# Gate table of a PEER layer built by 8 tokens instead of 4, with its products in alternating row blocks and one copy per PSUM bank

## The chip, the cores and the metric

One core of one Trainium2 chip runs the whole kernel. The metric is device time in microseconds; the time of a kernel is the median of its runs.

## The reference

One inference step of a two-layer encoder for 256 prompt rows and 128 sample rows of width 1024. Layer 0 mixes with a short gated convolution, layer 1 with stick-breaking attention; after each follows a PEER channel mixer, and every sub-layer ends in a layer norm. What matters here is PEER, for 256 rows at a time:

```python
q = (xb @ w_q).reshape(PEER_BLOCK, PEER_HEADS, 2, PEER_HALF)
s = jnp.einsum("thpc,hpnc->thpn", q, subkeys)
s_top, i_top = lax.top_k(s, K)
cand = s_top[:, :, 0, :, None] + s_top[:, :, 1, None, :]
cand_idx = i_top[:, :, 0, :, None] * PEER_N_KEYS + i_top[:, :, 1, None, :]
best, pos = lax.top_k(cand.reshape(PEER_BLOCK, PEER_HEADS, K * K), K)
expert = jnp.take_along_axis(cand_idx.reshape(...), pos, axis=-1)
g = jax.nn.softmax(best, axis=-1)
act = jax.nn.gelu(jnp.einsum("td,thkd->thk", xb, u_tab[expert]), approximate=False)
return jnp.einsum("thk,thkd->td", g * act, v_tab[expert])
```

Each token has 8 heads with 16 experts each, so 128 chosen experts of 16384, numbered 128 x + y by a first key x and a second key y.

## The kernel before, in words

The 128 sample rows and the 256 prompt rows take two ways through the same engines. For the sample rows the chosen experts' rows are gathered from HBM (`peer_gather`, L354, L367, L372: a gather by GpSimd, then one pass of VectorE over each gathered tile of 128 x 1024). For the prompt rows all 16384 experts are computed, and a gate is zero where a token has not chosen the expert (`peer_dense`). Both run at the same time, and the sample rows' work fills VectorE and the DMA queues beside the prompt rows' work.

`peer_dense` has three stages in each of the two layers. First, 14 pairs of blocks of 128 experts get their first product early, while VectorE does the routing (`a_pair`, from L382). Second, the gate table G is built (L407 to L437); this is the stage that the change rewrites. Third, for 64 pairs of blocks, the first product, the gate's product (`wt`, L457) and the second product follow, with float32 operands split in two parts.

The gate table. G[j, group, t, i] is the gate of token t for expert (group * 16 + i, j). It is built from one-hot rows: with the 128 chosen experts of a token on the partitions, `oi` is the gate where i equals x and zero elsewhere, `oj` is one where j equals y, and `oj`^T `oi` sums them into 128 x 128 gates of one token. The comparisons come from products: TensorE forms i - x and (j - y)^2 for 4 tokens at a time as products with 18 rows of contraction (L422): `xj` holds x, y and two parts of y^2 of 4 tokens and two rows of ones, `near` the matching coefficients. The 18 rows lie in one of four blocks of 32 rows; q = t0 // 64 * 32 is that block, so 16 successive groups of 4 tokens use the same one. Each of the two products fills one PSUM bank of the pool `acc` (4 banks). VectorE makes `oi` from the first (L424), ScalarE `oj` from the second (L427), both from a PSUM bank of 512 columns. Four float32 products of 128 columns (L430), one for each token, fill a bank of the pool `pg` (2 banks); the profile has two records for each of them. Two ScalarE copies empty it: the first four groups go into G (L432), the last four into the tile `st` (L435; pool `ohp`, 3 buffers), which after every 8 tokens is stored to `Gd` in DRAM by the SP queue (L437). In the third stage, when G's first groups have been used, L459 reloads them from Gd.

`xj` is filled in `route_prompt`: the keys of one tile of 128 tokens go to DRAM (`xd`, L342) and come back, transposed, by two DMAs for each tile (L345).

The order. The code is written in program order, and the framework's scheduler decides at build time in which order each engine issues its instructions (`schedule_with_timeline_sim=True`): of what is ready by its own timing it takes what stands first in the program. A tile's slot in a pool is given out when an earlier user of it is done. On the chip each engine then works in that fixed order. The sample rows' attention is given a place in that order by `ranked`.

Of the kernel before, what the change touches and what calls it, by code (L numbers as in the profile page):

```python
# [18 lines left out]
P = 128  # L19
# [8 lines left out]
# those of them with (a + 1)(b + 1) <= 8, as (a's start and count, b's count): only they can be among the best 8  # L28
# [4 lines left out]
EARLY = 14  # pairs of blocks whose first product precedes the gates  # L33
KEEP = 4  # of them in SBUF until they are used, the others in DRAM
AHEAD = 4  # blocks by which the first product runs ahead of the second
# [3 lines left out]
def trunk(ctx: ExitStack, tc: tile.TileContext, I, O):  # L39
# [31 lines left out]
    with ExitStack() as es:  # L71
# [19 lines left out]
        # trig[k', k] = 1 where k' >= k  # L91
        nc.vector.tensor_scalar(trig, jp, 0.0, None, op0=OP.is_le)
        nc.vector.memset(ones, 1.0)
        # same[p, j] = 1 where p and j lie in the same block of 16
# [3 lines left out]
        # maskb[k, q]: 0 where k < q and both lie in the same block, else NEG or less  # L98
# [6 lines left out]
    def split(hi, lo, src):  # L105
        """src = hi + lo exactly, each of float32r's 12 significant bits"""
        nc.scalar.activation(hi, src, AF.Copy)  # L107
        return nc.vector.tensor_sub(lo, src, hi.bitcast(F32))  # L108
# [7 lines left out]
    def in_turn(this, that):  # L116
        """this behind that on their engine, which so changes its tables of functions less often"""
        tc.add_manual_dep(this.ins, that.ins.name, mybir.DependencyInfo(
            mybir.DependencyClass.NoSync, mybir.DependencyReason.SCHED_ONLY), reason="fewer loads of tables")
# [25 lines left out]
    def mm3(pt, L, R, first, last):  # L145
        """pt (+)= L^T R for operands in two parts"""
# [4 lines left out]
    def proj3(pt, w, hT, n):  # L151
        """pt[:, :n] = w^T hT, w: parts of 8 chunks of 128x128, hT: parts [128, 8, n]"""
        for c in range(NB):
            cs = slice(c * P, (c + 1) * P)
            mm3(pt[:, :n], [x[:, cs] for x in w], [x[:, c, 0:n] for x in hT], c == 0, c == NB - 1)

    def proj1(pt, w, hT):
        """pt = w^T hT in float32"""
# [34 lines left out]
    def transposed(r, dsts, ps):  # L193
        """write r^T into each of dsts (parts (hi, lo) [128, 8, 128], or one float32 tile)"""
# [15 lines left out]
    def topk_half(chains, small):  # L210
        """the 16 best of s [128, 128] and their places, in order; step by step for all chains (tv, ti, n, s)"""
# [12 lines left out]
    def stage2(tv, ti, al, g, e, nh=8):  # L224
        """experts e [128, 8, 16] (float32) and softmax gates g [128, 8, 16] of the 16 best pairs of each head.
        Only the pairs (a, b) with (a + 1)(b + 1) <= 16 can be among them: the others have 16 before them.
        tv: the best keys' values, and room behind them for as many numbers of keys"""
        # kind and head in one dimension: sums of values, then numbers of experts
# [29 lines left out]
        for k0, x, pl in ((0, ex8, places8), (8, ex, places)):  # L258
# [3 lines left out]
            # the numbers once for each rank, side by side  # L262
# [12 lines left out]
        # the sums of the cells: ever again the first half onto the second, in front of an odd one out  # L275
# [18 lines left out]
    def softmax(g, sm):  # L294
        """of each head's values less their maximum"""
# [5 lines left out]
    def from_pool(pl):  # L301
        """shapes count words of 4 bytes"""
        return lambda name, shape, dt=F32: pl.tile([P] + shape[:-1] + [shape[-1] * 4 // mybir.dt.size(dt)], dt, name=name)

    def from_arena(ar, start=0):
        """places in ar one after the other"""
# [13 lines left out]
    def route_prompt(tv, ti, al, xj, xd, gT, t):  # L320
        """of the 128 experts of tile t's tokens: the first keys x and the second keys y, as rows x, y and y^2 in two
        parts of 7 bits of every token, 4 tokens to a group and 16 groups to a block of 32 rows, into xj; the gates,
        into gT [128 k, 256 t]"""
# [19 lines left out]
        for b in range(2):  # L343
            p = (2 * t + b) * 32
            nc.sync.dma_start(xj[p:p + 16], xd[t, b * 64:b * 64 + 64].rearrange("(s r) (q k) -> (r q) s k", r=4, q=4))  # L345
# [5 lines left out]
    def gather(tab, ei, k):  # L351
        """rows of tab for the k-th experts of all tokens"""
# [26 lines left out]
    def peer_dense(L, hT, dn):  # L379
        """-> psum banks [2 tiles * 2 halves] of the sum over the experts"""  # L380
        lag, kept, early = {}, {}, {}

        def a_pair(i, pl, ps, native=False):
            """gelu(u h) of two blocks, with or without splitting u"""
# [11 lines left out]
        # some pairs while VectorE is busy with the routing  # L396
# [16 lines left out]
        # gates G[j, group, t, i] of the experts (group * 16 + i, j); the last four groups wait in DRAM  # L413
        G = dn.gp.tile([P, 4, TP, GI], F32, name="G")
        Gd = dram.tile([P, 4, TP, GI], F32, name="Gd")
        for t0 in range(0, TP, 4):
            us = slice(t0, t0 + 4)
            # i - x and (j - y)^2 of all places in a row and column, for 4 tokens
            q = t0 // 64 * 32
            px, pj = bank(acc), bank(acc)  # L420
            for k, pt in enumerate((px, pj)):
                nc.tensor.matmul(pt, lhsT=xj[q:q + 18, t0 % 64 // 4, :], rhs=near[q:q + 18, k, :], start=True, stop=True)  # L422
            oi = ohp.tile([P, 4, P], F32, name="oi")
            nc.vector.scalar_tensor_tensor(oi, px.rearrange("p (t i) -> p t i", i=P), 0.0,  # L424
                                           gT[:, us, None].to_broadcast([P, 4, P]), op0=OP.is_equal, op1=OP.mult)
            oj = ohp.tile([P, 4, P], F32, name="oj")
            nc.scalar.activation(oj.rearrange("p t j -> p (t j)"), pj, AF.Relu, bias=1.0, scale=-1.0)  # L427
            pt = bank(pg)
            for t in range(4):
                nc.tensor.matmul(pt[:, t * P:(t + 1) * P], lhsT=oj[:, t, :], rhs=oi[:, t, :], start=True, stop=True)  # L430
            ptv = pt.rearrange("p (t h g i) -> p h g t i", h=2, g=4, i=GI)
            nc.scalar.activation(G[:, :, us, :], ptv[:, 0], AF.Copy)  # L432
            if t0 % 8 == 0:
                st = ohp.tile([P, 4, 8, GI], F32, name="st")
            nc.scalar.activation(st[:, :, t0 % 8:t0 % 8 + 4, :], ptv[:, 1], AF.Copy)  # L435
            if t0 % 8 == 4:
                nc.sync.dma_start(Gd[:, :, t0 - 4:t0 + 4, :], st)  # L437
# [6 lines left out]
        for s in range(-AHEAD, NBLK, 2):  # L444
# [12 lines left out]
            nc.vector.tensor_mul(wt, lag.pop(s), G[:, g % 4, :, i:i + 2].rearrange("p t i -> p i t"))  # L457
            if i == GI - 2 and g < 4:
                nc.sync.dma_start(G[:, g], Gd[:, g])  # L459
# [3 lines left out]
            # the last two blocks by tiles, so that the first tile's normalization starts early  # L463
# [7 lines left out]
    def finish(pts, L_ln, hd, last, hT, hTf=None):  # L471
        """residual and layernorm of the two prompt tiles"""
        # the table of square roots, before the data is there
# [30 lines left out]
    def half_out(xT, name, n):  # L504
        """columns n * 512.. of x @ w, in psum"""
# [8 lines left out]
    def attn_sample(h):  # L514
        with ExitStack() as es:
# [8 lines left out]
            # block-diagonal queries [2 x 64 dims, (b, head, q)], and the mask in that order of columns  # L524
# [18 lines left out]
            # two pairs of heads at a time; columns of a pair: keys of the cache, new keys  # L543
# [366 lines left out]
```

## Time and profile before

| | us |
|---|---|
| median of 3 runs | 2388.8 (2382.14 to 2390.61) |
| span of the profiled execution, first to last instruction | 2374.8 |
| PE busy in it | 2271.8 |
| VectorE (DVE) busy | 1918.5 |
| ScalarE (ACT) busy | 1050.3 |

The list of times does not say which of them was the profiled execution; its own time is read from its span. PE is TensorE's matmuls, PEld its weight loads, SP the engine that issues most DMAs, L422 line 422 of the kernel. A matmul's record has a modelled end, so the start of the next is the surer number. DMA share is the mean busy share of 16 DMA engines.

### The profile page before, as it was taken

The page shows a single profiled execution, that of the slowest core. Times are in us where ns is not written, and L with a number is a line of the kernel's source. Part 1 is how long each engine was busy: PE and PEld are TensorE (multiplying, and loading weights), DVE is VectorE, ACT ScalarE, POOL GpSimd, SP SyncE. Part 2 cuts the span into 40 slices and gives each one's busy share as a digit, 9 for nine tenths or more (in the row PEclk, how much of TensorE's full clock was granted, in tenths as well). Part 3 has the DMA queues.
Part 4 walks back from the last instruction along what each step waited for, and adds up shares of the span by engine and source line. Part 5 has one row for each costly group of instructions (what it writes and reads, how often), then busy time and mean ns, then how long its engine had stood idle before and what let it go on. Part 6 is the DMA issues. An engine that isn't in the chain of part 4 may idle for free.

```text
span 2374.8 us, 37270 instructions
## 1 busy us (share of the span) xinstructions
PE 2271.8 (96%) x13708; PEld 1981.6 (83%) x13708; DVE 1918.5 (81%) x3493; ACT 1050.3 (44%) x1579; POOL 800.2 (34%) x659
## 2 busy tenths in 40 slices
PE   8979989999999999998799888988999999999997
PEld 8969876688888889887589677876698888888986
DVE  6559997898888889888623489987898888888888
ACT  3333325744444444443346432135644444444443
POOL 0002342353332343444221223443453332344442
PEclk9989998999999999999899999998999999999999
DMA  4556898999999999998976558989999999999996
GB/s 163 195 193 212 291 339 265 299 369 347 346 325 327 341 330 323 335 335 289 332 243 206 162 194 298 337 287 292 294 373 342 347 329 325 341 320 329 335 326 220
DMA packets 225928, 704.13 MB, mean 297 GB/s; under 512 B 24912, under 2 KB 59472, under 8 KB 224720
## 3 DMA queue, kind: packets, MB, share of 16 engines
q1 hardware_dynamic: 137200, 382.93, 45.3%
q0 software_dynamic: 87968, 318.28, 38.5%
q8 instruction: 108, 1.77, 0.3%
q14 instruction: 76, 0.62, 0.1%
q10 hardware_dynamic: 576, 0.52, 0.1%
HBM read 671.17 MB, written 30.48 MB: 295 GB/s over the span
## 4 chain that ended last, share of the span: by engine, by line
PE 80%; DVE 12%; DMA 5%; issue 2%; ACT 1%; POOL 0%; SPq 0%; DVEq 0%; ACTq 0%; POOLq 0%
PE acc L148 13%; PE acc L149 13%; PE acc L147 13%; PE pg L147 8%; PE pg L149 8%; PE pg L148 8%; PE pg L430 6%; PE ms L160 3%; PE acc L422 3%; DVE row L367 2%; DMA row<-in_pu,ei 2%; DMA row<-in_pv,ei 1%; PE ms L511 1%; DVE h L372 1%; DMA wv<-in_pvn 1%
## 5 line engine op out<-in xcount | busy, mean ns | idle before, releaser
L354 POOL DMA_INDIRECT row<-in_pv,ei x256 | 387.6, 1514 | 580.7 <-DVE h L372 448.4
L354 POOL DMA_INDIRECT row<-in_pu,ei x256 | 333.6, 1303 | 544.6 <-DVE row L367 409.4
L147 PE MATMUL pg<-hThi,uhi 128*128 128x256 f32 x1600 | 451.6, 282 | 0.0
L149 PE MATMUL pg<-hThi,ulo 128*128 128x256 f32 x1600 | 451.4, 282 | 0.0
L148 PE MATMUL pg<-hTlo,uhi 128*128 128x256 f32 x1600 | 451.3, 282 | 0.0
L108 DVE TENSOR_TENSOR vlo<-wv,vhi 128x1024 fp32r<-128x1024 f32 x280 | 341.9, 1222 | 89.4 <-ACT vhi L107 86.0
L107 ACT ACTIVATE vhi<-wv 128x1024 fp32r<-128x1024 f32 x280 | 295.3, 1055 | 259.9 <-PE acc L149 187.1
L148 PE MATMUL acc<-vlo,whi 128*128 128x512 f32 x1024 | 403.9, 394 | 0.1
L149 PE MATMUL acc<-vhi,wlo 128*128 128x512 f32 x1024 | 403.4, 395 | 0.0
L108 DVE TENSOR_TENSOR ulo<-wu,uhi 128x1024 fp32r<-128x1024 f32 x264 | 322.0, 1220 | 100.7 <-ACT uhi L107 91.0
L107 ACT ACTIVATE uhi<-wu 128x1024 fp32r<-128x1024 f32 x264 | 278.9, 1056 | 261.2 <-issue 92.5
L147 PE MATMUL acc<-vhi,whi 128*128 128x512 f32 x1024 | 345.5, 394 | 0.6 <-ACT whi L107 0.6
L372 DVE SCALAR_TENSOR_TENSOR h<-row,wg,h 128x1024 f32<-128x1024 f32 x256 | 327.4, 1279 | 18.7 <-DMA row<-in_pv,ei 18.3
L367 DVE SCALAR_TENSOR_TENSOR row<-row,h 128x1024 f32<-128x1024 f32 x256 | 310.5, 1216 | 13.8 <-DMA row<-in_pu,ei 13.7
L147 PEld LDWEIGHTS pg<-hThi,uhi 128*128 128x128 f32 x1600 | 304.7, 190 | 10.3
L148 PEld LDWEIGHTS pg<-hTlo,uhi 128*128 128x128 f32 x1600 | 304.7, 190 | 8.4
L149 PEld LDWEIGHTS pg<-hThi,ulo 128*128 128x128 f32 x1600 | 304.9, 191 | 5.3
L160 PE MATMUL acc<-arena,wu 128*128 128x256 f32 x1024 | 233.7, 387 | 17.3 <-DMA wu<-in_put 12.3
L160 PEld LDWEIGHTS acc<-arena,wu 128*128 128x128 f32 x1024 | 195.6, 194 | 49.7 <-DMA wu<-in_put 15.8
L149 PEld LDWEIGHTS acc<-vhi,wlo 128*128 128x128 f32 x1024 | 192.5, 188 | 40.3
L148 PEld LDWEIGHTS acc<-vlo,whi 128*128 128x128 f32 x1024 | 193.0, 188 | 37.5 <-DVE vlo L108 0.6
L147 PEld LDWEIGHTS acc<-vhi,whi 128*128 128x128 f32 x1024 | 187.8, 189 | 34.7 <-ACT whi L107 0.8
(261 smaller groups left out, 3244.7 us busy)
## 6 DMA issues: line engine op xcount, KB each, us to landing
wv<-in_pvn SPq DMA_DIRECT2D x256, 512.0 KB, 5.9
wu<-in_put SPq DMA_DIRECT2D x256, 512.0 KB, 6.2
row<-in_wpq POOLq DMA_DIRECT2D x32, 512.0 KB, 4.9
wu<-in_wpq SPq DMA_DIRECT2D x32, 512.0 KB, 5.2
Gd<-st SPq DMA_DIRECT2D x64, 256.0 KB, 5.4
G<-Gd SPq DMA_DIRECT2D x8, 2048.0 KB, 10.6
wu<-in_win SPq DMA_DIRECT2D x24, 512.0 KB, 3.5
early<-lag SPq DMA_DIRECT2D x20, 256.0 KB, 5.8
```

Source lines behind the costliest of these rows:

```text
L107: nc.scalar.activation(hi, src, AF.Copy)
L108: return nc.vector.tensor_sub(lo, src, hi.bitcast(F32))
L147: nc.tensor.matmul(pt, lhsT=L[0], rhs=R[0], start=first, stop=False)
L148: nc.tensor.matmul(pt, lhsT=L[0], rhs=R[1], start=False, stop=False)
L149: nc.tensor.matmul(pt, lhsT=L[1], rhs=R[0], start=False, stop=last)
L160: nc.tensor.matmul(pt, lhsT=w[:, c * P:(c + 1) * P], rhs=hT[:, c, :], start=(c == 0), stop=(c == NB - 1))
L354: nc.gpsimd.indirect_dma_start(out=row, out_offset=None, in_=tab, in_offset=bass.IndirectOffsetOnAxis(ap=ei[k // 32][:, k % 32:k % 32 + 1] ...
L367: nc.vector.scalar_tensor_tensor(u, u, 1.0, h, op0=OP.mult, op1=OP.mult, accum_out=dot[:, k:k + 1])
L372: nc.vector.scalar_tensor_tensor(r, v, wg[:, k:k + 1], r, op0=OP.mult, op1=OP.add)
L422: nc.tensor.matmul(pt, lhsT=xj[q:q + 18, t0 % 64 // 4, :], rhs=near[q:q + 18, k, :], start=True, stop=True)
L430: nc.tensor.matmul(pt[:, t * P:(t + 1) * P], lhsT=oj[:, t, :], rhs=oi[:, t, :], start=True, stop=True)
L511: nc.tensor.matmul(pt, lhsT=xT[:, c + i, :], rhs=w[:, i, :], start=(c + i == 0), stop=(c + i == 7))
```

## The change

The loop over 4 tokens becomes one over 8 tokens. The 4-token groups are dealt out over the four row blocks in turn, so two successive groups lie in different blocks; the loads of `xj` follow this, 4 for each tile instead of 2. All four distance products of the 8 tokens are written one behind the other, and take all four `acc` banks. One copy empties a whole `pg` bank: its output is a pattern of two pieces, the first four groups to their place in G, the last four to spare places for 16 tokens behind G's 256, in turns for even and odd steps. The store to Gd reads from there, and `st` is gone. G and the arena that shares its memory grow by 16 tokens. Comments and doc strings are removed all over the file, which is not shown.

```diff
-        for b in range(2):
-            p = (2 * t + b) * 32
-            nc.sync.dma_start(xj[p:p + 16], xd[t, b * 64:b * 64 + 64].rearrange("(s r) (q k) -> (r q) s k", r=4, q=4))
+        for b in range(4):
+            nc.sync.dma_start(xj[b * 32:b * 32 + 16, t * 8:t * 8 + 8],
+                              xd[t].rearrange("(s b r) (q k) -> b (r q) s k", b=4, r=4, q=4)[b])
...
-        G = dn.gp.tile([P, 4, TP, GI], F32, name="G")
+        G = dn.gp.tile([P, 4, TP + 16, GI], F32, name="G", tag="G")
         Gd = dram.tile([P, 4, TP, GI], F32, name="Gd")
-        for t0 in range(0, TP, 4):
-            us = slice(t0, t0 + 4)
-            q = t0 // 64 * 32
-            px, pj = bank(acc), bank(acc)
-            for k, pt in enumerate((px, pj)):
-                nc.tensor.matmul(pt, lhsT=xj[q:q + 18, t0 % 64 // 4, :], rhs=near[q:q + 18, k, :], start=True, stop=True)
-            oi = ohp.tile([P, 4, P], F32, name="oi")
-            nc.vector.scalar_tensor_tensor(oi, px.rearrange("p (t i) -> p t i", i=P), 0.0,
-                                           gT[:, us, None].to_broadcast([P, 4, P]), op0=OP.is_equal, op1=OP.mult)
-            oj = ohp.tile([P, 4, P], F32, name="oj")
-            nc.scalar.activation(oj.rearrange("p t j -> p (t j)"), pj, AF.Relu, bias=1.0, scale=-1.0)
-            pt = bank(pg)
-            for t in range(4):
-                nc.tensor.matmul(pt[:, t * P:(t + 1) * P], lhsT=oj[:, t, :], rhs=oi[:, t, :], start=True, stop=True)
-            ptv = pt.rearrange("p (t h g i) -> p h g t i", h=2, g=4, i=GI)
-            nc.scalar.activation(G[:, :, us, :], ptv[:, 0], AF.Copy)
-            if t0 % 8 == 0:
-                st = ohp.tile([P, 4, 8, GI], F32, name="st")
-            nc.scalar.activation(st[:, :, t0 % 8:t0 % 8 + 4, :], ptv[:, 1], AF.Copy)
-            if t0 % 8 == 4:
-                nc.sync.dma_start(Gd[:, :, t0 - 4:t0 + 4, :], st)
+        for t0 in range(0, TP, 8):
+            xy = [[bank(acc) for _ in range(2)] for _ in range(2)]
+            for k in range(2):
+                for n in range(2):
+                    q = (t0 // 4 + n) % 4 * 32
+                    nc.tensor.matmul(xy[k][n], lhsT=xj[q:q + 18, t0 // 16, :], rhs=near[q:q + 18, k, :],
+                                     start=True, stop=True)
+            for n in range(2):
+                t1 = t0 + 4 * n
+                oi = ohp.tile([P, 4, P], F32, name="oi")
+                nc.vector.scalar_tensor_tensor(oi, xy[0][n].rearrange("p (t i) -> p t i", i=P), 0.0,
+                                               gT[:, t1:t1 + 4, None].to_broadcast([P, 4, P]),
+                                               op0=OP.is_equal, op1=OP.mult)
+                oj = ohp.tile([P, 4, P], F32, name="oj")
+                nc.scalar.activation(oj.rearrange("p t j -> p (t j)"), xy[1][n], AF.Relu, bias=1.0, scale=-1.0)
+                pt = bank(pg)
+                for t in range(4):
+                    nc.tensor.matmul(pt[:, t * P:(t + 1) * P], lhsT=oj[:, t, :], rhs=oi[:, t, :], start=True, stop=True)
+                there = TP + t0 // 8 % 2 * 8 + 4 * n
+                both = bass.AP(tensor=G.tensor, offset=G[:, 0, t1:t1 + 4, :].offset,
+                               ap=[list(G.ap[0]), [(there - t1) * GI, 2], [(TP + 16) * GI, 4], [1, 4 * GI]])
+                nc.scalar.activation(both, pt.rearrange("p (t h g i) -> p h g t i", h=2, g=4, i=GI), AF.Copy)
+            nc.sync.dma_start(Gd[:, :, t0:t0 + 8, :], G[:, :, there - 4:there + 4, :])
...
-            nc.vector.tensor_mul(wt, lag.pop(s), G[:, g % 4, :, i:i + 2].rearrange("p t i -> p i t"))
+            nc.vector.tensor_mul(wt, lag.pop(s), G[:, g % 4, 0:TP, i:i + 2].rearrange("p t i -> p i t"))
             if i == GI - 2 and g < 4:
-                nc.sync.dma_start(G[:, g], Gd[:, g])
+                nc.sync.dma_start(G[:, g, 0:TP], Gd[:, g])
...
-            self.arena = self.gp.tile([P, 4 * TP * GI], F32, name="arena", tag="G")
+            self.arena = self.gp.tile([P, 4 * (TP + 16) * GI], F32, name="arena", tag="G")
```

## Rows read from the trace of the kernel before

**Rows 1.** The page's first part: busy time, share of the span, instructions.
```profile
span 2374.8 us, 37270 instructions
PE 2271.8 (96%) x13708; PEld 1981.6 (83%) x13708; DVE 1918.5 (81%) x3493; ACT 1050.3 (44%) x1579; POOL 800.2 (34%) x659
```

**Rows 2.** Stretches: length, busy us of each engine, PEclk, DMA share, GB/s.
```profile
400.00:480.00 80.00, 80.00 (x515) 56.28 (x515) 69.21 (x98) 54.87 (x143) 33.39 (x34) 1.00 0.98 300
1645.00:1720.00 75.00, 75.00 (x474) 51.33 (x474) 65.24 (x107) 53.48 (x142) 29.10 (x31) 1.00 0.95 299
```

**Rows 3.** PE in order of time, 429 to 437: start, us, line, form, count.
```profile
431.06 0.60 PE L422 MATMUL acc<-near,xj 18*128 18x512 bf16 x2
431.59 1.16 PE L430 MATMUL pg<-oi,oj 128*128 128x128 f32 x8
432.68 0.60 PE L422 MATMUL acc<-near,xj 18*128 18x512 bf16 x2
```

**Rows 4.** Groups of instructions, 420 to 460: busy us, mean ns, idle before.
```profile
L427 ACT ACTIVATE oj<-acc 128x512 f32<-128x512 f32 x25 | 15.1, 603 | 0.0
L422 PE MATMUL acc<-near,xj 18*128 18x512 bf16 x50 | 14.6, 380 | 0.0
```

**Rows 5.** PE in order of time, prompt attention, around 1184 and 1228.
```profile
1183.98 0.70 PE L667 MATMUL pg<-qkp 64*128 64x256 f32 x2
...
1228.54 0.71 PE L667 MATMUL pg<-qkp 64*128 64x256 f32 x4
```

**Rows 6.** PE in order of time, 395.9 to 399.5.
```profile
395.67 0.37 PE L422 MATMUL acc<-near,xj 18*128 18x512 bf16 x1 [0.32 <-ACT oj L427]
395.97 2.05 PE L430 MATMUL pg<-oi,oj 128*128 128x128 f32 x16
397.95 0.60 PE L422 MATMUL acc<-near,xj 18*128 18x512 bf16 x2
```

**Rows 7.** ACT in order of time, 429 to 437.
```profile
431.16 0.38 ACT L432 ACTIVATE G<-pg 128x256 f32<-128x256 f32 x1 [0.47 <-PE pg L430]
431.44 0.38 ACT L435 ACTIVATE st<-pg 128x256 f32<-128x256 f32 x1
431.71 0.60 ACT L427 ACTIVATE oj<-acc 128x512 f32<-128x512 f32 x1
```

**Rows 8.** All engines in order of time, 369.6 to 370.6.
```profile
369.73 0.60 ACT L427 ACTIVATE oj<-acc 128x512 f32<-128x512 f32 x1
...
370.41 0.50 PEld L430 LDWEIGHTS pg<-oi,oj 128*128 128x128 f32 x2 [0.84 <-ACT oj L427]
```

**Rows 9.** The tile Gd, its 24 stores issued from 400 to 480.
```profile
DMA to landing us min/median/max: 4.3/5.4/6.8
```

**Rows 10.** The stretch 381.6 to 396, columns as in rows 2.
```profile
381.60:396.00 14.40, 14.09 (x62) 9.83 (x60) 8.31 (x11) 6.97 (x19) 3.48 (x4) 0.66 0.56 164
```

**Rows 11.** The tile Gd, its 3 stores issued from 381.6 to 393.
```profile
DMA to landing us min/median/max: 2.6/2.6/2.9
```

**Rows 12.** The line of the xj loads, 340 to 365 (ns min/median/max of issuing).
```profile
L345 SPq DMA_DIRECT2D xj<-xd x4: 319/382/702, 354.9 to 357.9; - x4
  PE acc L422: 1.2, 1
```

**Rows 13.** PE in order of time, 381.5 to 386.8.
```profile
382.07 3.78 PE L430 MATMUL pg<-oi,oj 128*128 128x128 f32 x16
```

**Rows 14.** Stretches early in the stage, columns as in rows 2.
```profile
364.00:374.00 10.00, 10.00 (x36) 6.89 (x36) 6.81 (x9) 5.09 (x12) 1.88 (x2) 0.50 1.03 379
381.20:391.00 9.80, 9.80 (x38) 7.24 (x36) 4.11 (x5) 3.88 (x11) 1.88 (x2) 0.50 0.60 182
```

**Rows 15.** The SP queue's DMA issues at the end: sample rows, then prompt rows.
```profile
2360.10 0.34 SPq L838 DMA_DIRECT2D out_y<-h  x1
2369.59 1.66 SPq L484 DMA_DIRECT2D out_y<-wu  x2
```

## The prediction

> **What bounds the kernel now.** I read the page's summary first, then the table of stretches, then the time order of single engines inside the stage that the change rewrites. The summary has TensorE (PE) busy for nearly all of the span [rows 1]. The stretches show that this holds without a gap where the gate tables are built: PE is busy for all of 80 us in layer 0 and all of 75 us in layer 1, at the full clock, while VectorE (DVE) and ScalarE (ACT) have idle time left [rows 2]. So the question is what one step of this stage costs PE.
>
> PE's time order answers it [rows 3]. For each 4 tokens it shows two distance products (L422), then the 8 records of the four products of one-hot rows (L430; each float32 product leaves two records), then again L422. From one L422 pair to the next is 432.68 - 431.06 = 1.62 us: 0.53 until the first L430 and 1.09 until the next pair. For 8 tokens that is 3.24 us, and nothing in it is a wait: the pair of the next 4 tokens stands ahead of the L430 of these, because four acc banks hold two pairs. 64 steps of 8 tokens (32 in each layer) at 3.24 make 207 us of the span. Only these can move much.
>
> **Removed from PE.** In the new code two L422 that follow each other read different row blocks. The prompt attention in this same trace has both cases [rows 5]: two products in one row block last 0.70 us together, four in two row blocks (the same two, twice) 0.71. The second block rides along. So four L422 should take PE as long as two now, 0.53 to the first L430. The 16 L430 of a step then can stand together. Such a run of 16 exists: from its first to the next L422 is 397.95 - 395.97 = 1.98 us [rows 6]. PE's need is 0.53 + 1.98 = 2.51 for 8 tokens, taken as 2.55, against 3.24. If PE stayed the bound, 64 x 0.69 = 44 us would go. I do not think that it stays the bound.
>
> **Added: a round trip through ACT.** A step now takes all four acc banks. The next step's products get a bank only when `oi` or `oj` of this step has read it, and L430 of this step is ahead of them in program order. Before, the pair that L430 needs was a whole group old. I expect PE to run a step's second pair of L422, wait for `oj`, run 16 L430, and only then run the next such pair. Row by row: L422 0.37 and 0.05 until ACT starts, `oj` 0.60 [rows 4, 7], 0.08 from its end to L430 (369.73 + 0.60 to 370.41) [rows 8], 1.98 for 16 L430: 3.08 us. In ACT's order the last copy of the step before comes first: as now it starts 0.10 after the first L422 [rows 3, 7], and a copy of 512 columns should take what `oj` takes, 0.60. It ends at 0.70, where `oj` wanted to start at 0.42, so up to 0.28 is added: 3.08 to 3.36. PE itself already shows such a wait for `oj` at one place (0.32 before an L422) [rows 6]. The middle, 3.22, is what a step costs now: the side-by-side products are paid back as a wait.
>
> **One copy instead of two.** Two copies of 256 columns start 0.28 apart and take 0.38 each [rows 7], 0.66 together; one of 512 takes 0.60 by `oj`. ACT saves 0.06 for each 4 tokens. ACT is idle for 31% of the stage [rows 2], so I cost this at nothing; if ACT were the limit it would be 8 us. The 512-column copy writes pieces of 256 bytes; no row has just that pattern on ACT, and I bound it between 0.60 and 0.76 (two copies with no overlap).
>
> **Two landing places instead of three.** `st` had three buffers; the 16 spare tokens of G are two. The first copy of a step must wait until the store of two steps before has landed, and everything behind it on ACT, `oj` of the next step included, waits too. The store lands 5.4 us after issue in the median, 4.3 to 6.8 [rows 9]. One place then turns over in 5.4 plus the two copies that fill it (0.60 + 0.49, since ACT starts the next some 0.1 us before the end) plus about 0.07: 6.56 us for two steps, 3.28 for one. At 4.3 it is 2.73, at 6.8 3.98. With three buffers the store had a step more, and no wait shows. Stores land faster only where DMA is little used: 2.6 us in the median [rows 11] at a share of 0.56 [rows 10]; in the stage the share is 0.98 [rows 2], because the sample rows' gathers run on. I take the median.
>
> So a step has two cycles of nearly the same length, 3.22 and 3.28, and the later one wins in each turn; the landings scatter by over 1 us. I take 3.35, a little above both. 64 x (3.35 - 3.24) = 7 us more.
>
> **The smaller edits.** The key table xj is loaded by 8 DMAs instead of 4 in each layer. SP issues one in 0.38 us and PE waited 1.2 us for them in layer 0 [rows 12]; at worst 4 x 0.38 = 1.5 us a layer stand in front of the first product, at best nothing, since the first step needs two of them alone. I take 1 us for both layers. G is 4 KB longer in each partition and `st` is gone: no time. The gate's read and the reload of G only get a limit on tokens: no time, as each touches the same elements.
>
> **Sum.** 7 + 1 = 8 us more. The profiled execution has a span of 2374.8 us; the median of the runs, 2388.8, lies 14.0 above it, which I take as what surrounds a span. 2374.8 + 8 + 14 = **2397 us**.
>
> **One rule against the change.** The rows say that four acc banks hold two pairs now and one step then. The Trainium skill, TensorEngine Tiling (Array Packing), section Restrictions and Gotchas, says the same as a warning: row tiling raises PSUM pressure, since each row tile needs its own bank. The same page, section Performance Considerations, expects the copies out of PSUM to become the bottleneck after the speedup; by that ACT would set the step at 4 x 0.60 = 2.4 us, under PE's 2.55, and the stage would gain. No row here decides between that and the round trip above.
>
> **Rivals.** *Faster (0.27):* the compiled order puts the next products between the two L430 groups of a step, so that `oj` is ready early, and the stores land at the quick end. PE's 2.55 is then held by the places at 2.73: 64 x 0.51 = 33 us less, 2357. For it: order is chosen by a planner, and at 395.97 it put 16 L430 together. Against: banks come free late, and 4.3 is the shortest of 24 landings [rows 9]. A larger gain would meet the sample rows, whose output is issued 9.5 us before the prompt's last [rows 15].
>
> *Slower, the landing places (0.22):* the store's landing decides every step. The point is 2 x 3.24 - 1.16 = 5.3 us; above it the stage is longer than now, and the median is just there. At 6.1, half way to the longest, a step is 3.63: 64 x 0.39 = 25, 2415 with the edits. For it: a late copy holds back `oj` behind it, so that one late landing is not caught up.
>
> *Slower, the clock (0.08):* early in the stage the granted clock fell to half twice, with PE busy by its records [rows 14], and there 16 L430 took 3.78 us instead of 2.05 [rows 6, 13]. With a wait in each step it could fall again. A quarter of the steps at half clock costs 16 x 1.73 = 28 us: 2425. Against: from 400 us on it stayed full. The Trainium skill, TensorE: Matmul & The Clock Gate, section A second HAM failure mode: psum-queue depth-cycling, tells of short PE waits between groups, from cycling through PSUM banks, that make the clock swing; by that rule this rival is the likely one, and the rows of the first 30 us bear it out, those after do not.
>
> *Much slower (0.03):* the framework sees the spare places as one piece, and each copy waits for the store just before: 6.56 a step, 64 x 3.32 = 212, about 2602.
>
> That the products do not run side by side is inside the forecast: PE would need 2.55 + 0.46 = 3.01, still under 3.22.
>
> **The numbers.** Forecast 0.40. A measurement of this kernel can tell about 0.5%, 12 us, from no change: the bounds are 2377 and 2401. Faster 0.27 plus the forecast's lower tail, 0.28; slower 0.22 + 0.08 + 0.03, less a little of the first that stays under 2401, 0.32; same 0.40. The range 2355 to 2432 leaves out the last rival, half of the clock's and the far end of the faster one, some 0.17 together. As both signs have weight: the forecast's own range is 2380 to 2412.
>
> **What would show it.** Right: PE idle for some 0.6 us in each step before L430, released by `oj`; a step of about 3.35 us between first L422s; ACT's copies waiting for the landing of the Gd store; L422 starting in twos. Wrong: PE busy throughout and steps under 3.0 us (faster rival); a step of twice the landing; or copies that never wait for a store, with half clock in the stretches.

## The result and the profile after

The changed kernel takes 2479.3 us in the median of 4 runs (2464.4 to 2482.9), the kernel before 2385.8 beside it: a ratio of 1.0385 with a 95% interval of 1.0348 to 1.0422. It is slower by 93 us, outside the predicted range. The ratios here and below leave out runs more than 1.5% above the fastest run of the same kernel, the medians do not. The page of the changed kernel, against [rows 1]:

```profile
span 2474.8 us, 37201 instructions
PE 2297.4 (93%) x13708; PEld 2016.4 (81%) x13708; DVE 1924.4 (78%) x3493; ACT 1045.5 (42%) x1454; POOL 753.5 (30%) x659
```

The span grew by 100.0 us and PE's busy time by 25.6, so some three quarters of the loss is PE standing still. Where? The distance products mark the two gate stages. The line's own answer has first and last start (fifth and sixth number), layer 0 and then layer 1, first of the kernel before, then of the changed one (L422 is now L423, L430 is L435, the one copy is L439, `oj` L432, `oi` L428, the store L440):

```profile
L422 PE MATMUL acc<-near,xj x128: 371/384/629, 360.1 to 471.4; 18*128 18x512 bf16 x128
L422 PE MATMUL acc<-near,xj x128: 371/384/626, 1599.3 to 1716.3; 18*128 18x512 bf16 x128
```

```profile
L423 PE MATMUL acc<-near,xj x128: 371/384/629, 416.1 to 544.5; 18*128 18x512 bf16 x128
L423 PE MATMUL acc<-near,xj x128: 371/384/629, 1692.7 to 1815.3; 18*128 18x512 bf16 x128
```

Five differences make the 100 us. Until the first product: 360.1 to 416.1, **+56.0**. Layer 0's stage: 111.3 to 128.4, **+17.1**. From there to layer 1's stage: 1127.9 to 1148.2, **+20.3**. Layer 1's stage: 117.0 to 122.6, **+5.6**. The rest: 658.5 to 659.5, +1.0. So 76 us were lost where no changed line of the gate stage runs, most of them before the first one ran.

Stretches before the stage show the place (columns as in [rows 2]), first of the kernel before, then of the changed one, which also has its two stages:

```profile
220.00:240.00 20.00, 19.67 (x170) 19.48 (x170) 20.00 (x97) 5.58 (x13) 6.02 (x9) 1.00 0.56 189
240.00:260.00 20.00, 20.00 (x130) 18.65 (x129) 19.48 (x96) 5.37 (x9) 7.91 (x7) 1.00 0.85 294
360.00:474.00 114.00, 112.26 (x643) 76.25 (x644) 91.83 (x123) 75.05 (x193) 38.32 (x42) 0.91 0.92 281
```

```profile
220.00:240.00 20.00, 1.83 (x7) 1.25 (x6) 18.12 (x65) 1.96 (x5) 11.09 (x11) 0.50 0.83 275
240.00:260.00 20.00, 8.55 (x38) 8.25 (x39) 17.37 (x43) 3.44 (x8) 12.66 (x12) 0.59 0.86 293
416.00:547.00 131.00, 110.91 (x658) 80.63 (x656) 102.51 (x144) 70.36 (x130) 51.86 (x50) 0.87 0.91 289
1693.00:1819.00 126.00, 107.70 (x661) 78.86 (x658) 101.66 (x146) 71.58 (x132) 48.37 (x49) 0.89 0.91 297
```

From 220 to 260 PE was busy for 39.7 of 40 us and is now for 10.4, at half to six tenths of the clock. The longest wait of the changed kernel from 165 to 280 names the cause (sum, times, longest):

```profile
PEld pg L725 <- ACT q L720: 29.8, 2, 24.2
```

L720 copies the prompt rows' queries `q`, from which their keys are chosen. L725 is PE's product of them with the subkeys. PE stands for 24 us waiting for the first of the copies. ACT in order of time shows what had to come first:

```profile
243.97 0.23 ACT L273 ACTIVATE pf<-pos 128x32 bf16<-128x32 uint32 x1 [7.33 <-DVE g L274]
244.21 1.28 ACT L296 ACT_TABLE_LOAD   x1
245.50 0.31 ACT L296 ACTIVATE g<-g 128x128 f32<-128x128 f32 x1
245.72 0.37 ACT L720 ACTIVATE q<-acc 128x256 f32<-128x256 f32 x1
255.44 0.66 ACT L720 ACTIVATE q<-acc 128x256 f32<-128x256 f32 x2 [9.35 <-DVE e L288]
```

L273 and L296 are the end of the *sample* rows' routing, and the prompt rows' `q` needs nothing of its results. The first copy stands behind them in ACT's compiled order. The second waited 9.35 us for L288, which is that routing too. In the kernel before the same copy (L717) started at 169.4 and ran beside the sample rows' routing; this is its row there, then here (copies up to 320 us):

```profile
L717 ACT ACTIVATE q<-acc x16: 364/366/384, 169.4 to 250.7; 128x256 f32<-128x256 f32 x16
```

```profile
L720 ACT ACTIVATE q<-acc x14: 365/367/385, 245.7 to 307.8; 128x256 f32<-128x256 f32 x14
```

What the two share is memory. 16 more tokens make the arena 4 x 16 x 16 x 4 = 4096 bytes longer in each partition, and every pool laid out behind it moves up by as much, `q`'s among them. The temporary pools of the sample rows' routing grow from the other end. In the layout of the built program `q` ended 1152 bytes below them before, and lies over them now. A slot of `q` is then given out when the last user of the tiles under it is done. Under the first slot that is L274, which released L273 above; under the second it is L288. `st` lived in a pool that is opened later, so that its going did not help here.

The stage itself also has other lines than forecast. PE in order of time, in layer 0, and then the copies of the same moments in ACT's order:

```profile
521.59 2.05 PE L435 MATMUL pg<-oi,oj 128*128 128x128 f32 x16 [1.34 <-ACT G L439]
523.57 0.39 PE L423 MATMUL acc<-near,xj 18*128 18x512 bf16 x2
525.00 1.16 PE L435 MATMUL pg<-oi,oj 128*128 128x128 f32 x8 [1.04 <-ACT G L439]
```

```profile
520.94 1.08 ACT L439 ACTIVATE G<-pg 128x512 f32<-128x512 f32 x2 [1.42 <-DMA Gd<-G]
524.35 1.08 ACT L439 ACTIVATE G<-pg 128x512 f32<-128x512 f32 x2 [1.84 <-DMA Gd<-G]
```

Two products in two row blocks last 0.39 us together, where two in one block took 0.60 [rows 3]: they do run side by side. But PE now stands before L435 for 1.34 and 1.04 us, released by the copy, and the copy by the store's landing. Over the stage the waits are:

```profile
ACT oj L432 <- PE acc L423: 31.6, 22, 6.3
PEld pg L435 <- ACT G L439: 14.8, 21, 1.8
ACT G L439 <- DMA Gd<-G: 6.6, 7, 1.8
```

PE is idle for 20.1 of 131 us of the stage and 18.3 of 126, by the stretches; before it was 1.7 of 114 and 9.2 of 120. The mean clock tells the time at half clock as well, twice what it lacks of 1: 2 x 0.13 x 131 = 34 us, against 2 x 0.09 x 114 = 21 before, both in layer 0.

### The profile page after: what moved, and what is told of

Same layout as the page of the kernel before. It is cut to its first block, busy times and chain, and to the rows that moved or that the text cites. A ratio compares the mean times of both kernels' runs of the same rounds, so it can differ in the third digit from the quotient of the medians.

```text
span 2474.8 us, 37201 instructions
## 1 busy us (share of the span) xinstructions
PE 2297.4 (93%) x13708; PEld 2016.4 (81%) x13708; DVE 1924.4 (78%) x3493; ACT 1045.5 (42%) x1454; POOL 753.5 (30%) x659
## 4 chain that ended last, share of the span: by engine, by line
PE 58%; issue 15%; DVE 12%; DMA 8%; POOL 5%; ACT 2%; POOLq 0%; SPq 0%; DVEq 0%; ACTq 0%
PE acc L147 10%; PE acc L149 10%; PE acc L148 10%; PE pg L147 6%; PE pg L149 6%; PE pg L148 6%; POOL row L354 4%; DMA Gd<-G 3%; PE pg L435 3%; DMA row<-in_pu,ei 3%; PE ms L160 2%; DVE row L367 2%; DVE h L372 2%; ACT G L439 1%; PE acc L423 1%
## 5 line engine op out<-in xcount | busy, mean ns | idle before, releaser
L354 POOL DMA_INDIRECT row<-in_pv,ei x256 | 345.0, 1348 | 584.9 <-DVE h L372 401.0
```

The source lines that it names most:

```text
L354: nc.gpsimd.indirect_dma_start(out=row, out_offset=None, in_=tab, in_offset=bass.IndirectOffsetOnAxis(ap=ei[k // 32][:, k % 32:k % 32 + 1] ...
```

## The experiments

Twelve kernels were run, in four groups; each ratio is to runs of the kernel before on the same chip (2381.6, 2383.5, 2382.4 and 2384.6 us in the four groups). "Stages" below are from first distance product to last gate product, layer 0 and layer 1; before: 113.7 and 119.4 us.

### The memory: key tiles moved, the table longer alone, and both

The changed kernel with nothing altered but the place of three small key tiles, which go to the part of the arena that the 16 tokens added; all behind them, `q` too, comes back to its old place:

```diff
-            self.best = [(al(f"tv{t}", [32, 16]), al(f"ti{t}", [16, 16], U32)) for t in range(2)]
+            end = from_arena(self.arena, 4 * (TP + 16) * GI - 1024)
+            self.best = [((end, al)[t](f"tv{t}", [32, 16]), end(f"ti{t}", [16, 16], U32)) for t in range(2)]
```

> The change as it is, but three of the four tiles of best keys (4 KB in each partition) lie in the free end of the arena, so that the tiles of the prompt's key choice (pool bk) get back the addresses that they had before, clear of the sample routing's tiles. Theory (the longer table pushed bk's q tiles onto memory that the sample routing still uses, so the prompt's key choice waited for the sample routing to end): the gate stage of layer 0 starts at about 361 us again instead of 422, that of layer 1 gains some 20 us more, and the time falls by 60 to 85 us, to 2395 to 2420. Rival (the planner came to another order because of the new stage itself or of the eight xj loads): the start stays near 422 us and the time within 10 us of the changed kernel's 2479.

Measured: 2419.4 us, ratio 1.017 (1.0122 to 1.0218). The row of `q`:

```profile
L720 ACT ACTIVATE q<-acc x16: 362/367/384, 168.6 to 249.9; 128x256 f32<-128x256 f32 x16
```

It starts at 168.6 again, and the first distance product is back at 360.9. The opposite edit gives the kernel before a longer table and arena, and nothing else (the table's readers keep to its first 256 tokens, which is not shown):

```diff
-        G = dn.gp.tile([P, 4, TP, GI], F32, name="G")
+        G = dn.gp.tile([P, 4, TP + 14, GI], F32, name="G")
...
-            self.arena = self.gp.tile([P, 4 * TP * GI], F32, name="arena", tag="G")
+            self.arena = self.gp.tile([P, 4 * (TP + 14) * GI], F32, name="arena", tag="G")
```

> The kernel before, with nothing changed but the length of the arena and of G: 14 tokens (3.5 KB in each partition) that nothing uses. bk's q tiles then lie over the sample routing's tiles, as in the changed kernel. Theory (memory alone): slower than before by 60 to 90 us, 2445 to 2475, the first product of the gate stage near 420 us. Rival (the new stage or its loads): within 5 us of before, 2381 to 2391.

Measured: 2452.1 us, ratio 1.0299 (1.0252 to 1.0346), with no operation added, removed or moved by the edit:

```profile
L717 ACT ACTIVATE q<-acc x14: 366/372/388, 261.9 to 310.0; 128x256 f32<-128x256 f32 x14
```

The control puts two of the key tiles of that kernel into its arena's unused end, which leaves `q` 3584 - 3072 = 512 bytes above its old place:

```diff
-            self.best = [(al(f"tv{t}", [32, 16]), al(f"ti{t}", [16, 16], U32)) for t in range(2)]
+            end = from_arena(self.arena, 4 * (TP + 14) * GI - 768)
+            self.best = [((end, al)[t](f"tv{t}", [32, 16]), (end, al)[t](f"ti{t}", [16, 16], U32)) for t in range(2)]
```

> The kernel before with the table and the arena longer by 14 unused tokens (alone: 2452.1 us, 70 more than before), and with the first key tiles tv0 and ti0 in the arena's unused end, so that the prompt's key tiles come back clear of the memory of the sample rows' routing. My theory, the shared memory is the whole price of the longer table: the first distance product of layer 0 returns from 414.7 to about 360 us, and the time to within 10 us of before, 2374 to 2394. Rival, the longer table costs something else beside (the arena's other strides, the stretched reload, another order of the instructions): over 2405, with the first distance product back at 360 or not.

Measured: 2385.0 us, ratio 1.0002 (0.9971 to 1.0033), and

```profile
L717 ACT ACTIVATE q<-acc x16: 364/367/385, 170.6 to 251.8; 128x256 f32<-128x256 f32 x16
```

So a longer table costs nothing that these runs can tell (the interval is 8 us either way), and its overlap 70 us: 512 bytes do no harm, as they fit into the 1152 that were free, 3584 do. This part is settled from both sides.

### The landing places: three, two and one

The run with the key tiles moved (two places, 2419.4 us) is the base of the next six. Three places of 8 tokens need 2 KB more; all four key tiles go to the arena's end, and, to make room, three of the early first products are kept on the chip instead of four (KEEP); 24 stands wherever the table's length had 16:

```diff
-KEEP = 4
+KEEP = 3
...
-                there = TP + t0 // 8 % 2 * 8 + 4 * n
+                there = TP + t0 // 8 % 3 * 8 + 4 * n
```

> As e1_keys_in_arena, with three spare landing places of 8 tokens in turn instead of two (all four tiles of best keys in the arena's end; 3 early pairs instead of 4 stay in SBUF, which gives the 2 KB for it). Theory (landing places cost what ACT's copies wait for them in e1, 12.6 us in the stage of layer 0, and as much in layer 1): no wait of the copies for the store, 15 to 25 us less than e1, 2395 to 2404. Rival (that wait only stands in for the wait on the banks): within 8 us of e1.

Measured: 2373.5 us, ratio 0.9962 (0.9938 to 0.9985): 46 us for one more place, more than was expected. As two edits stand in it, one run had the second alone:

```diff
-KEEP = 4
+KEEP = 3
```

> This is the run with the key tiles in the arena's free end (two landing places, 2419.4 us), with one thing altered: three tiles of early first products are kept instead of four, as in the run with three landing places (2373.5). It tells whether the 46 us between those two came from the third landing place or from the smaller number of kept tiles. My theory, landing places: within 6 us of 2419, so 2413 to 2426, with copies that wait for the store to land and half clock in both gate stages as before. Rival, the kept tiles: 2375 to 2400, with the gate stages as in the run with three places (109 and 112 us between first distance product and last gate product).

Measured: 2416.4 us, ratio 1.0138 (1.0112 to 1.0165). By the runs beside them, it lies 34.0 us above the kernel before, the one with three places 10.1 below: the place is worth some 44. The control's six runs scatter by 34 us, from 2400 to 2434, so this is known to within some 10 us. And one place less:

```diff
-                there = TP + t0 // 8 % 2 * 8 + 4 * n
+                there = TP + 4 * n
```

> The run with the key tiles in the arena's free end, with one landing place of 8 tokens instead of two, so that each step's first copy must wait for the store of the step just before. My theory, the landing decides the step: one place turns over in 5.4 us of landing plus 1.16 us for the copies, 6.56 us for each 8 tokens, 32 times in a layer: 210 us for a gate stage instead of 129 and 135, so 2419 + 156 = 2575 us, at the stores' quick end of 4.3 us (5.46 x 32 = 175 a stage) 2505. Rival, the round trip of oj and oi through four banks decides and the landing only comes in now and then: under 40 us more, 2420 to 2460, with stages below 150 us. By the theory the copy waits in nearly all of the 32 steps, by the rival in fewer than half.

Measured: 2594.2 us, ratio 1.0875 (1.0836 to 1.0913), near the 2575 of the theory. The copies of two steps in ACT's order (rows between left out), and then who waited for the tile Gd in the first stage (us, times):

```profile
502.99 1.09 ACT L439 ACTIVATE G<-pg 128x512 f32<-128x512 f32 x2 [3.09 <-DMA Gd<-G]
509.29 1.09 ACT L439 ACTIVATE G<-pg 128x512 f32<-128x512 f32 x2 [0.69 <-DMA Gd<-G]
```

```profile
  ACT G L439: 52.7, 30
```

From one step's copies to the next is 6.30 us, where the prediction worked out 6.56 for one turn of a place, and 30 of the stage's 32 steps wait; over the stage a step takes 215.9 / 32 = 6.7 us. The stretches of both stages, for three places, two and one:

```profile
359.00:469.00 110.00, 99.00 (x643) 73.81 (x644) 95.76 (x130) 71.12 (x130) 45.66 (x45) 0.92 0.97 311
1611.00:1723.00 112.00, 106.27 (x663) 79.01 (x663) 92.97 (x142) 72.10 (x132) 39.72 (x42) 0.89 0.91 298
```

```profile
360.00:490.00 130.00, 113.74 (x641) 82.08 (x641) 103.13 (x142) 70.89 (x129) 50.70 (x52) 0.83 0.91 290
1623.00:1759.00 136.00, 110.49 (x663) 79.84 (x662) 106.01 (x152) 71.01 (x133) 53.58 (x54) 0.87 0.92 294
```

```profile
364.00:581.00 217.00, 150.34 (x640) 111.87 (x640) 158.03 (x199) 73.10 (x129) 105.88 (x94) 0.58 0.86 275
1713.00:1938.00 225.00, 149.47 (x656) 113.73 (x656) 162.24 (x221) 73.78 (x130) 108.24 (x97) 0.64 0.85 279
```

With two places instead of three the stages are 44 us longer, which is all of the difference. PE's idle time is 41.8 instead of 16.7 us, and its busy time 224.2 instead of 205.3: 25 + 19 = 44. The busy part has two sources. PE's time at half clock is 80 us instead of 42, by the mean clock, and 16 records of the gate products took 3.78 us at half clock instead of 2.05 [rows 6, 13]. And the compiled order is another one, with two places and then with three (rows between left out):

```profile
459.03 1.16 PE L435 MATMUL pg<-oi,oj 128*128 128x128 f32 x8
460.12 0.39 PE L423 MATMUL acc<-near,xj 18*128 18x512 bf16 x1
461.53 0.60 PE L423 MATMUL acc<-near,xj 18*128 18x512 bf16 x3
462.06 1.16 PE L435 MATMUL pg<-oi,oj 128*128 128x128 f32 x8
```

```profile
424.84 1.16 PE L435 MATMUL pg<-oi,oj 128*128 128x128 f32 x8
425.93 0.39 PE L423 MATMUL acc<-near,xj 18*128 18x512 bf16 x2
427.66 1.16 PE L435 MATMUL pg<-oi,oj 128*128 128x128 f32 x8
```

In many steps with two places the four distance products stand as one and three between the groups of gate products, and a step without a wait takes 462.06 - 459.03 = 3.03 us; with three places they stand as two and two, and it takes 427.66 - 424.84 = 2.82. How much of the 19 is the clock and how much the order isn't told apart. The copies' own waits for the landing are a small part of the 44, 12.6 us in layer 0's stage with two places. ACT with two places, the first copy of each of six steps (rows between left out):

```profile
431.51 1.08 ACT L439 ACTIVATE G<-pg 128x512 f32<-128x512 f32 x2 [1.08 <-DMA Gd<-G]
434.77 1.08 ACT L439 ACTIVATE G<-pg 128x512 f32<-128x512 f32 x2 [0.51 <-DMA Gd<-G]
438.08 1.08 ACT L439 ACTIVATE G<-pg 128x512 f32<-128x512 f32 x2 [0.48 <-DMA Gd<-G]
441.68 1.09 ACT L439 ACTIVATE G<-pg 128x512 f32<-128x512 f32 x2 [0.84 <-DMA Gd<-G]
444.40 1.13 ACT L439 ACTIVATE G<-pg 128x512 f32<-128x512 f32 x2
449.22 1.09 ACT L439 ACTIVATE G<-pg 128x512 f32<-128x512 f32 x2 [1.75 <-DMA Gd<-G]
```

The steps are 3.26, 3.31, 3.60, 2.72 and 4.82 us. Three are as long as forecast, but the late landing's step adds more than the short one gives back: 3.54 in the mean. Over the whole stage the mean is higher, 129.2 / 32 = 4.0.

### The banks

The rival to the landing places was the round trip through four `acc` banks. The pool `ms` has two banks that are free in this stage; the second products go there, first with two places, then with three:

```diff
-            xy = [[bank(acc) for _ in range(2)] for _ in range(2)]
+            xy = [[bank(ps) for _ in range(2)] for ps in (acc, ms)]
```

> As e1_keys_in_arena, with the second products of a step in the two banks of the pool ms, which nothing else uses in this stage: first products have four banks, two steps of them, and the round trip through oj is out of PE's way. Theory (a step waits on the banks, and PE's waits bring the half clock): PE's idle time in the stages, 15 and 25 us in e1, falls below 8 us, the half clock in them from 44 and 34 us below 25, and the time by 25 to 40 us, to 2380 to 2395. Rival (landing places decide): within 8 us of e1.

Measured: 2419.4 us, ratio 1.0152 (1.0099 to 1.0205): no gain. My theory fell here, and the landing places were left as what decides.

> Three landing places and six banks together. If the two waits are separate costs, their gains add up: 40 to 60 us under e1, 2360 to 2380, below the kernel before. If they stand in for each other, it is like the better of the two.

Measured: 2363.9 us, ratio 0.9932 (0.9903 to 0.9961), stages of 101.9 and 103.7 us. Against three places alone that is 10 us less by the medians and 7 by the ratios, whose intervals overlap. So the banks gain something only once the landing does not hold the step, and how much is known only roughly.

### The products: same block, and a loop that keeps the old distance

With two places, both groups of a step put back into one row block (the loads of `xj` as before the change):

```diff
-                    q = (t0 // 4 + n) % 4 * 32
-                    nc.tensor.matmul(xy[k][n], lhsT=xj[q:q + 18, t0 // 16, :], rhs=near[q:q + 18, k, :],
+                    q = t0 // 64 * 32
+                    nc.tensor.matmul(xy[k][n], lhsT=xj[q:q + 18, t0 % 64 // 4 + n, :], rhs=near[q:q + 18, k, :],
```

> The first kernel of this call (keys in the arena) with both groups of a step in the same row block and the two loads of xj for each tile of before: the products don't run side by side. Theory (a step is a round trip through ACT and a landing place, PE has idle time in it): within 10 us of the first kernel. Rival (PE sets the step): 64 x 0.45 = 29 us slower than the first kernel.

Measured: 2452.5 us, ratio 1.0307 (1.0264 to 1.0349), 33 us more than with two blocks. My theory, that the waits hide it, is refuted. The stretches of its stages:

```profile
361.00:515.00 154.00, 145.75 (x643) 97.47 (x644) 99.42 (x135) 72.78 (x130) 47.85 (x48) 0.69 0.78 232
1655.00:1796.00 141.00, 126.16 (x658) 87.55 (x656) 110.02 (x156) 73.06 (x131) 60.49 (x56) 0.84 0.91 294
```

PE is idle for less time than with two blocks, 23.1 us against 41.8, but 95 us of layer 0's stage are at half clock. How much of the 33 us is the longer products and how much the clock isn't told apart by this run.

The next two leave the loop at 4 tokens, the copies and `st` as before, take the new loads of `xj`, and alter which two products stand together: (j - y)^2 of one group beside i - x of the next, in another row block:

```diff
+        oi = None
+        for n in range(TP // 4 + 1):
+            pair = [(k, m, bank(acc)) for k, m in ((1, n - 1), (0, n)) if 0 <= m < TP // 4]
+            for k, m, pt in pair:
+                q = m % 4 * 32
+                nc.tensor.matmul(pt, lhsT=xj[q:q + 18, m // 4, :], rhs=near[q:q + 18, k, :], start=True, stop=True)
+            was = oi
```

> The kernel before, with its 4-token loop, its two copies, st and its memory, and two edits: groups of 4 tokens in alternate row blocks, and the second product of one group issued beside the first product of the next. The four acc banks then still hold two pairs. If PE sets the stage before (1.62 us for 4 tokens, nothing in it a wait) and the pair costs what one product costs: 128 x 0.22 = 28 us less than before, 2358, unless the sample rows' gathers or ACT hold it. If a round trip through ACT comes in here too (oj is needed one group sooner): no gain, 2380 to 2400.

Measured: 2368.3 us, ratio 0.9957 (0.9934 to 0.998), stages of 112.0 and 108.8 us. PE in order of time:

```profile
430.90 0.39 PE L422 MATMUL acc<-near,xj 18*128 18x512 bf16 x2
431.25 1.13 PE L437 MATMUL pg<-oi,oj 128*128 128x128 f32 x8
432.31 0.39 PE L422 MATMUL acc<-near,xj 18*128 18x512 bf16 x2
```

A group of 4 tokens takes 1.41 us here, against 1.62 in [rows 3]: this is the idea of the change without its waits. 128 groups would give 27 us; 13 came out by the medians, 10 by the ratio. With the second products in the `ms` banks (`bank((acc, ms)[k])` in that line):

> As e4_neighbours, with the second products in the two banks of ms, so that three pairs are in flight. If VectorE's order (gathers' rows between the oi) is what holds PE in e4, more banks let PE run ahead over it: 5 to 10 us under e4, 2358 to 2363. If the 1.41 us for 4 tokens of PE is the bound already: within 4 us of e4.

Measured: 2365.0 us, ratio 0.9921 (0.9895 to 0.9948), stages of 104.4 and 100.8 us. Last, this loop with three landing places, one copy of 512 from a bank and the key tiles in the arena's end:

```diff
-            ptv = pt.rearrange("p (t h g i) -> p h g t i", h=2, g=4, i=GI)
-            nc.scalar.activation(G[:, :, us, :], ptv[:, 0], AF.Copy)
+            there = TP + t0 % 24
+            both = bass.AP(tensor=G.tensor, offset=G[:, 0, us, :].offset,
+                           ap=[list(G.ap[0]), [(there - t0) * GI, 2], [(TP + 24) * GI, 4], [1, 4 * GI]])
+            nc.scalar.activation(both, pt.rearrange("p (t h g i) -> p h g t i", h=2, g=4, i=GI), AF.Copy)
```

> Three things that each gained alone, in one kernel: the loop by 4 tokens with (j - y)^2 of one group issued beside i - x of the next in another row block, on six banks (2365.0), and the three landing places with one copy of 512 columns from a bank, with all key tiles in the arena's free end (2373.5, with six banks 2363.9). First theory, they stack: ACT saves its second copy in each step, a step of 4 tokens stays at 1.41 us where nothing waits, stages of 95 to 102 us, 2350 to 2362. Rival, the sample rows' gathers and VectorE beside the stage now bound it, and what the products gain no longer comes out: within 6 us of 2364, stages of 101 to 105 us. A third way, the landings wait again as each 512-column copy needs its place: over 2370, with copies waiting for the store in the stage.

Measured: 2376.0 us, ratio 0.9939 (0.9909 to 0.997), which is some 2368 us beside the kernel before. The interval, 2361 to 2375, has its middle where the rival put it and touches the ranges of the other two. The gains don't stack in full, and why stays open. The quickest kernels are this loop on six banks (0.9921) and the changed loop on six banks with three places (0.9932); the runs don't tell these two apart, and both beat the kernel before, by less than 1%.

## Why the prediction was wrong

The step that failed is the sentence "G is 4 KB longer in each partition and `st` is gone: no time". It had no row and no bound. Measured, it is the largest term: 70 us with the loop of before, and 56 with the changed one (93.5 us above before with it, 37.9 without). Of the 76 us that the trace shows outside the stage to which the whole sum was confined, 55 before the first product and 10 between the stages go when the key tiles are moved (360.9 and 1138.7 us, for 416.1 and 1148.2). The other 10 between the stages are not shown to be a cost: the run with the longer table and moved key tiles has 1138.2 there too, against 1127.9, and is no slower than before. No rival had this term, so no part of the range reached it.

The three prices add up by the runs beside each: +56 for the memory, +48 for two places instead of three (37.9 + 10.1, of which some 4, less than the runs can tell, may be the kept tiles), and -10 for what is left, the products side by side and the one copy: +94, as it must be, against 93.5 measured.

*PE's need, and the products side by side.* The products do run side by side, 0.39 us for two, and the copy of 512 columns took the 0.60 us that was forecast. But the need of 2.55 us for 8 tokens was too low. It rested on 16 gate product records standing together, and in many steps the compiled order puts distance products between the two groups of 8: a step without a wait takes 2.82 or 3.03 us (rows above). That order is also the first condition of the faster rival, and no gain came with it. The aside that products one behind the other would be "inside the forecast" was wrong: 33 us.

*Two landing places.* The mechanism was right and the turn nearly so: 6.56 us was worked out, 6.30 stands in the rows with one place and 6.7 in the mean of that stage, and steps of 3.26 to 3.60 in the run with two. The size was off. Taking a typical 3.35 a step gave +7 us; with the memory mended the two stages are 264.3 us instead of 233.1, +31. PE's idle time in them, 41.8 us instead of 10.9, is all of it; its busy time is 224.2 instead of 223.1, so that nothing is left of what the products save side by side. What the sum lacked is the tail, late landings that short steps don't make good: the stores landed after 2.6 to 7.7 us there, 5.8 and 5.3 in the median of the two stages, and the longest that the sum allowed for was 6.8. I wrote that a late copy holds back `oj` behind it, and put that into a rival of 0.22 instead of the sum; that rival's 2415 is near the 2419.4 with the memory mended.

*The round trip through the banks.* Counted as a cycle as long as the landing's. Six banks gave nothing with two places and 7 to 10 us with three, so it is the shorter of the two. The sign "PE idle before L430, released by `oj`" came out mostly as released by the copy L439. The Trainium skill, TensorEngine Tiling (Array Packing), section Restrictions and Gotchas, was cited for its warning on banks; here that pressure is real but came second.

*The clock rival (0.08).* Half clock did come more often, 34 us against 21 in layer 0's stage, worth some 7 us of PE's work there. With the memory mended it is 80 us against 37 over both stages, some 21 us of work: the rival's direction was right, and its 28 us not far off. The Trainium skill, TensorE: Matmul & The Clock Gate, section A second HAM failure mode: psum-queue depth-cycling, ties it to short waits of PE between groups; three runs agree, with a mean clock of 0.92 for three places, 0.83 for two and 0.58 for one in layer 0's stage, while PE's idle time goes from 11 to 16 to 67 us. Others do not. The run in one row block has 0.69 at 8 us of idle time. The control with two places and three kept tiles has 0.92 at 19 us in layer 0's stage and 0.62 at 21 in layer 1's. And [rows 14], which the prediction took as support for that rule, have half clock with PE busy throughout. What sets the clock in this stage stays open.

*The edits of xj, 1 us.* The run with the neighbours' loop has all 8 loads, and its first distance product starts at 357.2 us against 360.1 before, so that no delay shows; they were not measured alone.

*The 14 us around the span.* The profiled run of the changed kernel took 2476.65 us with a span of 2474.8, so that 1.8 us surround a span; the rest of the 14 is scatter between runs. The sum starts from the median either way, so that this did no harm.

## What to carry to other kernels

A change of a tile's size is a change of the memory layout: list what lies behind it and what grows towards it, and ask of each pair that now overlaps which work was running at the same time. Only that concurrency is lost, so the cost shows as a wait on work that the waiting instruction needs nothing of, far from the edit. And when a buffer's turnover (landing plus filling) is as long as the time until it is needed again, count it as too short: price the late landings, and the clock, not the median.

## What was not expected of the hardware

Two products of 18 rows in two row blocks take 0.39 us where one takes 0.37 to 0.38 [rows 4]: the second is all but free, at 18 rows of contraction too. And waits are not the whole price of a late store: with one landing place the copies waited 52.7 us for stores in layer 0's stage, while the stage is 102 us longer than before (215.9 against 113.7), with 2 x 0.42 x 217 = 182 us of it at half clock.
